# TensorE in source order: projections taken in set numbers between the steps of linear attention and attention

## The chip, the cores and the metric

The kernel runs on one core of one Trainium2 chip. TensorE (PE) multiplies, VectorE (DVE), ScalarE (ACT) and GpSimd (POOL) work element by element, SyncE (SP) and the other queues start DMAs. Each engine takes its instructions in the order in which they stand in its own queue and waits on semaphores for the others. The metric is the time of one execution on the device in microseconds; a kernel's time is the median of its runs. Beside it stands one profiled execution, from which all rows below come.

## The reference

A two-layer encoder for one sequence of 512 tokens with 16 learned meta tokens ahead of them (528 in all, width 1024). Each layer is a feed-forward half step, a mixer and another half step; the mixer runs gated linear attention and softmax attention side by side and merges them by gates.

```python
for l in range(DEPTH):                     # DEPTH = 2
    h = h + 0.5 * swiglu(rmsnorm(h, g[l, 0]), gate[l, 0], up[l, 0], down[l, 0])
    h = h + mixer(rmsnorm(h, g[l, 1]), w_in[l], ...)
    h = h + 0.5 * swiglu(rmsnorm(h, g[l, 2]), gate[l, 1], up[l, 1], down[l, 1])
return rmsnorm(h, final_norm)[:, N_META:]

def mixer(z, ...):
    q_a, k_a, v_a, r_a, lr_f, lr_b, q_b, k_b, v_b, g_a, g_b = split(z @ w_in)
    a = gla_branch(...)        # 4 heads (keys 64, values 128), forwards and backwards, chunked, decay per channel:
                               # o_t = q_t . S_t,  S_t = diag(alpha_t) S_{t-1} + k_t^T v_t; RMS norm per head; * silu(r_a)
    b = attention_branch(...)  # 8 query heads, 2 key heads of 64; RMS norm of q and k, rotary positions, softmax
    y = sigmoid(g_a + b0) * (a @ w_pa) + sigmoid(g_b + b1) * (b @ w_pb)
    return y @ w_out
```

In the last layer only the 512 tokens are needed behind the mixer's keys and values.

## The kernel before

Everything is held as channels by tokens: the 1024 channels are 8 chunks of 128 partitions, the 528 tokens lie along the free dimension, and a matmul takes a 128x128 weight tile and 264 tokens (512 where only the tokens count). Each float32 product is three matmuls on split operands: `whi` (ScalarE's cast, L222) and `wlo` (the remainder, L223 on VectorE) of the weights with the same two of the activations. `Weights` keeps a plan of all tiles in order of use, fetches them in slabs of 512 KB by DMA on SyncE's queue and makes `whi` and `wlo` four slabs ahead.

Feed-forward blocks take the gate and up products in pairs of blocks by seven products in place of eight (`product_of_pair`, matmuls at L498), then the down product (`product`, L378). `Norm` prepares the next block as chunks of the residual `h` are finished: `pair` splits the operands (`xc`, L429 and L430), `square` adds up the squares (L412, L416), and `rs` takes the mean over channels on TensorE (`means`, L384) and the inverse root.

The mixer projects four `r`, the low-rank decays `lr`, and then, pair of heads by pair of heads, `q`, `k` and two `v` (`project`, matmuls at L378, evacuated by L465). `gla_pair` works on one pair: the decays for both directions (L608 to L642: a product with `w2`, exponentials and logarithm on ScalarE, cumulative sums L618 on VectorE), products of keys and queries with the decays (L644, L647, L664), transposes (L596, L651), the chunk states (L687 to L702), scores inside a chunk with their mask (L714 to L718), outputs (L723, L724, copied by L726), and the norm per head (square L731, mean L384, logarithm L390, exponential L361, then L734 and L735). `attention` projects keys, values and queries, normalises and rotates them (`rope`, L743 to L746), and its `prologue(g)` prepares one group of four query heads: means of the query squares (L796, L798), their inverse roots `rq` (L803 to L808), and the queries split into a high and a low half (L818, L819). `group` walks through 8 units a group: four score matmuls for each of two heads (L832, L833), maximum (L835), exponential (L361), scaling, transposes (L857, L867), copies (L860, L861), and products with the values (L874, L875). 16 projections for the gates end in `g` (copied by L578, scaled by L951).

The source says what is computed; the order on every engine is set by the tile framework's scheduler, which by its own costs draws matmuls of any step forward as soon as their operands and buffers allow. So projections stand between the transposes and scores where it put them. The late 12 gates of a layer take their `wlo` from POOL (`W.lo = G`) instead of VectorE, and so does the product `kp` (L645) in `gla_pair`.

Of the kernel before, what the change touches and what calls it, by code (L numbers as in the profile page):

```python
# [29 lines left out]
EARLY = 4  # L30
KINDS = ("ss", "mm", "ss", "sm")
AHEAD = 1
SLAB = 1024
# [14 lines left out]
def ffn_steps():  # L48
# [3 lines left out]
    for g, n in enumerate(GROUPS):  # L52
        steps += [("P", pair, c) for c in "1265"]
# [14 lines left out]
def weight_plan():  # L68
# [8 lines left out]
    def ffn(l, f):  # L77
        for step in ffn_steps():
            if step[0] == "P":
                plan.append(("op", (l, f)) + step[1:])  # L80
            else:
                _, g, m, first, last = step
                mat("ffn_w_down", (l, f), m * P, 2 * sum(GROUPS[:g]) + first, last - first)

    gate_cols = [c + m * P for m in range(KC) for c in (O_GA, O_GB)]
    for l in range(DEPTH):
# [8 lines left out]
        for c in gate_cols[:EARLY] + [O_KB, O_VB] + [O_QB + i * P for i in range(4)] + gate_cols[EARLY:]:  # L95
            mat("w_in", (l,), c, 0, KC)
# [153 lines left out]
def build(tc, ctx, xt, wts, win, par, w2, const, umask, out):  # L250
# [129 lines left out]

    def means(weights, x):
# [16 lines left out]
    class Norm:  # L398


        def __init__(self, gc):
            self.gc, self.x, self.acc = gc, [], None
# [14 lines left out]

        def pair(self, j):

            raw = [slot("t"), slot("t")]  # L420
            for i, t in enumerate(raw):
                S.activation(t, h(2 * j + i), AF.Identity, scale=col(self.gc + 2 * j + i))
# [26 lines left out]
        def chunk_of_pair(self, c):  # L449
            self.square(c)  # L450
            if c % 2:
                self.pair(c // 2)

# [24 lines left out]
    def ffn(l, f, norm, done, following):  # L478
# [6 lines left out]
        def product_of_pair(p, product):  # L485
# [4 lines left out]
            if begin:  # L490
                st[where] = pair(kind == "s2")
            acc = st[where][:, :, :w]
            hi, lo = W.op((l, f), p, product)
            at = PLACE[product]
            for k, (xh, xl) in enumerate(x):
                for j in range(2):
                    for i, (a, b) in enumerate(((hi, xh), (hi, xl), (lo, xh))):
                        TE.matmul(acc[:, j], a[:, j, k], b[:, at], start=bool(begin and k == 0 and i == 0),  # L498
                                  stop=k == len(x) - 1 and i == 2, skip_group_check=not begin)
# [58 lines left out]
        for i, step in enumerate(steps):  # L558
            if step[0] == "P":
                product_of_pair(*step[1:])  # L560
                if step[1:] == (0, "5"):
                    rs = norm.rs()
# [9 lines left out]
    def project(x, rs, tag, f=1.0, n=T):  # L572
        t = slot(tag, n=n)
        acc = product("w_in", Acc("mm", n), x, KC, by_half=True)
        with tc.high_priority():
            if rs is None:
                for pv, cut in acc.parts:
                    S.copy(cut(t), pv)  # L578
            else:
                scaled(t, acc, rs, f)  # L580
        return t
# [4 lines left out]
    def gla_pair(l, p, lr, w2t, sr, qa, ka, va, n_out):  # L586

        prods = []
        qin = None
        dec = small.tile([P, 2, NB], F32, tag="dec", name=nm("dec"))  # L590
        kt, vk = [slot("q"), slot("q")], [slot("q"), slot("q")]
        ktm = slot("k")
        for hh in range(2):
            tp = pair()
            for b, bs, _ in blocks:
                TE.transpose(tp[:, 0, bs], va[hh][:, bs], ident)  # L596
            TE.transpose(tp[:META, 1, :P], va[hh][:, MB], ident)
            S.copy(vk[hh][:, :SEQ], tp[:, 0])
            S.copy(ktm[:META, 256 + hh * P : 256 + (hh + 1) * P], tp[:META, 1, :P])

        def blk(ap):
            return ap[:, :SEQ].rearrange("p (b t) -> p b t", b=NB)

        for d in range(2):
# [4 lines left out]
            a, g, c, ct_ = slot("t"), slot("t"), slot("t"), slot("t")  # L609
# [11 lines left out]
            mm_, mt_ = c[:, T - 1 : T].broadcast_to([P, META]), None  # L621
# [9 lines left out]
            qp, kp = slot("p"), slot("p")  # L631
            if d == 0:
                S.activation(g, a, AF.Exp, scale=-r16)
                S.activation(a, a, AF.Exp, scale=r16)
                S.activation(c, c, AF.Exp, scale=r16)
                S.activation(ct_, ct_, AF.Exp, scale=-r16)
                ein, eq, ek, eend = c, a, g, ct_
            else:
                S.activation(c, a, AF.Exp, scale=-r16)
                S.activation(a, a, AF.Exp, scale=r16)  # L640
                S.activation(ct_, ct_, AF.Exp, scale=-r16)
                S.activation(g, g, AF.Exp, scale=r16)  # L642
                ein, eq, ek, eend = ct_, c, a, g
            V.tensor_tensor(qp[:, :n_out], qa, eq[:, :n_out], ALU.mult)  # L644
            G.tensor_tensor(kp, ka, ek, ALU.mult)  # L645
            ke = slot("p")
            V.tensor_tensor(ke, ka, eend, ALU.mult)  # L647

            tp = pair()
# [8 lines left out]
            if qin is None:  # L658
                qin = [slot("p"), slot("p")]
            e0 = 127 if d == 0 else 0  # L660
            for hh in range(2):
                rows = slice(hh * HD, (hh + 1) * HD)
                to = slice(d * HD, (d + 1) * HD)
                V.tensor_tensor(qin[hh][to, :n_out], qa[rows], ein[rows, :n_out], ALU.mult)  # L664
                V.tensor_copy(dec[to, hh, :], blk(ein)[rows, :, e0])
            prods.append((qp, kp))
# [9 lines left out]

# [7 lines left out]
        for b in [NB, 0, 1, 2, 3]:  # L684
# [5 lines left out]
            if b == NB:  # L690
                S.copy(state(0)[0:HD], pv[0:HD])
            elif b < NB - 1:
                for hh in range(2):
                    V.scalar_tensor_tensor(state(nxt)[0:HD, hh], state(b)[0:HD, hh], dec[0:HD, hh, b : b + 1],
                                           pv[0:HD, hh], ALU.mult, ALU.add)
            if b != NB:
# [393 lines left out]
```

## Time and profile before

| | before |
|---|---|
| median of 3 runs (lowest to highest) | 2320.05 us (2318.82 to 2320.76) |
| profiled execution, its span | 2324.93 us, 2323.2 us |
| TensorE busy, mean granted clock | 2244.2 us (97%), 0.983 |
| VectorE, ScalarE, POOL busy | 1525.0 us, 1192.3 us, 231.8 us |
| HBM read | 264.38 MB |

The span runs from the first to the last instruction of the profile; the profiled execution's own time is 1.7 us longer and 4.9 us above the median. Layer 0's first feed-forward block lies at 34 to 390 us, its mixer to 830, the second block to 1182, layer 1's first block to 1556, its mixer to 1968, the last block to the end. Rows of instructions read: line, engine, operation, output<-inputs, shapes, count, then busy time, mean duration in ns, and the idle time before with what ended it. A duration runs from an instruction's start to its end; the next one on the same engine can start before that.

### The profile page before, as it was taken

Reading aid. Unit: us, or ns where it says so; the run is one execution under the profiler, and the core shown is the slowest. Engines: PE = TensorE matmul, PEld = TensorE weight load, DVE = VectorE, ACT = ScalarE, POOL = GpSimd, SP = SyncE. Lnnn points to the kernel's source line nnn. Section 1 sums busy time; section 2 is a strip of 40 time slices with the busy share of each in tenths; the row PEclk is TensorE's granted clock in tenths of the full one; section 3 lists DMA queues with packets and bytes.
Section 4 is the critical chain, followed back from the end, with each engine's and each line's share of the span. In section 5 each row is a group of like instructions: output and inputs, shape, how many; then the busy total and the mean of one; then the engine's idle time right before and its main releaser. Section 6 shows DMA issues by size and latency. Waiting matters only on the chain.

```text
span 2323.2 us, 39861 instructions
## 1 busy us (share of the span) xinstructions
PE 2244.2 (97%) x16548; PEld 2122.3 (91%) x16548; DVE 1525.0 (66%) x2355; ACT 1192.3 (51%) x1761; POOL 231.8 (10%) x218
## 2 busy tenths in 40 slices
PE   6999999999899999999989999999998999999997
PEld 5999999989899999999989999998787878989896
DVE  6657567566875676565676565674768767656666
ACT  7536354344784464453565353553446846636353
POOL 1111000000112010101011110100001110101010
PEclk9999999999998999999989999999999999999999
DMA  8868563111103386776658585632121135958671
GB/s 230 233 160 219 140 158 106 64 48 64 37 28 100 102 204 167 186 186 173 170 139 209 147 219 144 172 101 73 46 64 45 32 124 140 229 150 215 160 178 64
DMA packets 88412, 315.19 MB, mean 136 GB/s; under 512 B 9830, under 2 KB 12262, under 8 KB 88232
## 3 DMA queue, kind: packets, MB, share of 16 engines
q1 hardware_dynamic: 61136, 218.26, 28.4%
q0 software_dynamic: 25344, 92.29, 22.4%
q8 instruction: 130, 2.13, 0.4%
q10 hardware_dynamic: 1752, 2.11, 0.3%
q14 instruction: 50, 0.41, 0.1%
HBM read 264.38 MB, written 2.10 MB: 115 GB/s over the span
## 4 chain that ended last, share of the span: by engine, by line
PE 89%; DVE 6%; ACT 2%; issue 1%; DMA 1%; SPq 0%; DVEq 0%; POOL 0%; ACTq 0%
PE ss L498 38%; PE ss L378 27%; PE mm L378 12%; PE sm L378 3%; PE sm L857 1%; PE sm L874 1%; PE ss L714 1%; PE sm L875 1%; DVE wlo L223 1%; PE ss L832 1%; PE ss L384 1%; PE sm L687 1%; PE ss L833 1%; ACT whi L222 1%; PE sm L723 1%
## 5 line engine op out<-in xcount | busy, mean ns | idle before, releaser
L498 PE MATMUL ss<-xc,whi 128*128 128x264 f32 (+1 forms) x4928 | 902.3, 285 | 25.5 <-ACT whi L222 9.2
L498 PEld LDWEIGHTS ss<-xc,whi 128*128 128x128 f32 x4928 | 766.8, 189 | 28.1 <-ACT whi L222 9.9
L498 PE MATMUL ss<-xc,wlo 128*128 128x264 f32 (+1 forms) x2464 | 702.0, 285 | 3.5 <-DVE wlo L223 3.5
L378 PE MATMUL ss<-g,whi 128*128 128x264 f32 (+2 forms) x2668 | 494.2, 301 | 0.0
L498 PEld LDWEIGHTS ss<-xc,wlo 128*128 128x128 f32 x2464 | 466.0, 189 | 4.6 <-DVE wlo L223 4.4
L378 PEld LDWEIGHTS ss<-g,whi 128*128 128x128 f32 x2668 | 388.6, 188 | 17.4
L378 PE MATMUL mm<-x,whi 128*128 128x264 f32 (+1 forms) x1712 | 387.0, 318 | 0.1
L222 ACT CAST whi<-w 128x1024 fp32r<-128x1024 f32 (+1 forms) x221 | 230.8, 1047 | 257.9 <-PE ss L378 116.0
L222 ACT CAST whi<-raw 128x1024 fp32r<-128x1024 f32 x190 | 199.2, 1048 | 303.0 <-PE mm L378 108.0
L223 DVE TENSOR_TENSOR wlo<-w,whi 128x1024 fp32r<-128x1024 f32 (+1 forms) x221 | 267.9, 1218 | 108.5 <-ACT whi L222 106.3
L378 PE MATMUL ss<-g,wlo 128*128 128x264 f32 (+2 forms) x1334 | 310.0, 301 | 0.0
L378 PEld LDWEIGHTS mm<-x,whi 128*128 128x128 f32 x1712 | 283.3, 192 | 19.8 <-issue 2.5
L378 PE MATMUL mm<-x,wlo 128*128 128x264 f32 (+1 forms) x856 | 269.9, 320 | 0.0
L223 DVE TENSOR_TENSOR wlo<-raw,whi 128x1024 fp32r<-128x1024 f32 x166 | 203.1, 1224 | 98.6 <-ACT whi L222 97.5
L378 PEld LDWEIGHTS ss<-g,wlo 128*128 128x128 f32 x1334 | 213.4, 188 | 8.7
L223 DVE TENSOR_TENSOR wlo<-s,whi 128x1024 fp32r<-128x1024 f32 x88 | 107.6, 1223 | 101.7 <-ACT whi L222 101.7
L378 PEld LDWEIGHTS mm<-x,wlo 128*128 128x128 f32 x856 | 162.8, 192 | 11.0 <-issue 2.2
L222 ACT CAST whi<-s 128x1024 fp32r<-128x1024 f32 x88 | 92.4, 1050 | 154.1 <-PE ss L498 134.4
L465 DVE SCALAR_TENSOR_TENSOR t<-ss,rs 128x528 f32<-128x528 f32 (+1 forms) x95 | 66.0, 700 | 126.9 <-PE ss L378 126.8
L173 ACT ACTIVATE s<-w 128x1024 f32<-128x1024 f32 x88 | 93.3, 1060 | 84.6 <-DMA w<-win 47.9
L223 POOL TENSOR_TENSOR wlo<-raw,whi 128x1024 fp32r<-128x1024 f32 x24 | 57.7, 2403 | 363.0 <-ACT whi L222 279.7
L178 POOL DMA_DIRECT2D s<-win x44 | 41.1, 934 | 508.7 <-ACT s L173 508.4
(234 smaller groups left out, 2747.9 us busy)
## 6 DMA issues: line engine op xcount, KB each, us to landing
w<-win SPq DMA_DIRECT2D x219, 512.0 KB, 4.6
raw<-wts SPq DMA_DIRECT2D x190, 512.0 KB, 3.4
s<-win POOLq DMA_DIRECT2D x44, 512.0 KB, 6.8
w<-s POOLq DMA_DIRECT2D x44, 512.0 KB, 5.7
w<-win POOLq DMA_DIRECT2D x44, 512.0 KB, 6.9
s<-w POOLq DMA_DIRECT2D x44, 512.0 KB, 7.1
h<-xt SPq DMA_DIRECT2D x3, 528.0 KB, 6.6
out<-h SPq DMA_DIRECT2D x4, 256.0 KB, 2.3
```

Of the source, the lines that this page charges most:

```text
L173: self.nc.scalar.activation(t, w, AF.Copy, scale=-1.0)
L178: self.nc.gpsimd.dma_start(t, src, accum_op=ALU.add)
L222: nc.scalar.copy(hi[:, cs], w[:, cs])
L223: self.lo.tensor_tensor(lo[:, cs], w[:, cs], hi[:, cs].bitcast(F32), ALU.subtract)
L378: TE.matmul(acc.half[i][:width], lhs, rhs[:, acc.spans[i]], start=first, stop=last)
L384: TE.matmul(a, weights, x[:, hs], start=True, stop=True)
L465: V.scalar_tensor_tensor(cut(dst[rows]), pv[rows], -0.5 * f, cut(rs[rows]), ALU.mult, ALU.mult)
L498: TE.matmul(acc[:, j], a[:, j, k], b[:, at], start=bool(begin and k == 0 and i == 0), stop=k == len(x) - 1 and i == 2, skip_group_check=no ...
L687: TE.matmul(ps[:, hh * P : (hh + 1) * P], ktok(b, hh), vtok(b, hh), start=True, stop=True)
L714: TE.matmul(ats[:n, hh, d * n : (d + 1) * n], prods[d][1][rows, bs], prods[d][0][rows, bs], start=True, stop=True)
L723: TE.matmul(os_, vtok(b, hh), t3[:, hh], start=True, stop=False)
L832: TE.matmul(s[:n, i, :HF], lhs, kh[:, hs], start=True, stop=False)
```

## The change

TensorE alone is put under `manual_schedule`: its instructions now issue in the order of the source; the other engines are still ordered by the scheduler. In the source, `project` becomes `projection`, a generator that yields after each matmul, and `Stream` runs 30 of them a layer (24 matmuls of 264 or 512 tokens in each half). `pump(n)` issues the next n matmuls (a 512-wide one counts two), and `get` runs the stream until a projection is done. `gla_pair`, `keys_values` (the keys' and values' part of `attention`) and `attention` call `pump` with set numbers; in the attention units `share()` spreads what is left over 96 across the units. The decays are a function of their own (`gla_decays`): those of pair 1 are computed in the middle of pair 0, ahead of its norm. Keys and values come before pair 1; all 16 gates come last. The splits of both branches' outputs move into the units of the second group (`between`). The `wlo` of the late gates and `kp` come back from POOL to VectorE, each half of a projection is evacuated by itself, the first two products behind a norm (`products_late`, and the first pair of a feed-forward block) take the last operand's matmuls last, and `chunk_of_pair` squares a chunk after its operands are split.

```diff
-    def project(x, rs, tag, f=1.0, n=T):
-        t = slot(tag, n=n)
-        acc = product("w_in", Acc("mm", n), x, KC, by_half=True)
...
+    def projection(key, x, rs, f=1.0, n=T):
+        cost = 2 if n == SEQ else 1
+        def run():
...
+                        TE.matmul(a, lhs, rhs[:, hs], start=k == 0 and i == 0, stop=k == KC - 1 and i == 2)
+                        if (k, i) != (KC - 1, 2):
+                            yield cost
+                with tc.high_priority():
+                    if rs is None:
+                        S.copy(t[:, hs], a)
+                    else:
+                        V.scalar_tensor_tensor(t[:, hs], a, -0.5 * f, rs[:, hs], ALU.mult, ALU.mult)
+                yield cost
+            return t
+        return key, run, cost * 3 * KC * (1 if n == SEQ else 2)
...
+    class Stream:
+        def pump(self, n):
+            while n > 0 and (self.current or self.jobs):
+                if self.current is None:
+                    key, run, _ = self.jobs.pop(0)
+                    self.current = key, run()
+                try:
+                    done = next(self.current[1])
+                    n -= done
+                    self.left -= done
+                except StopIteration as end:
+                    self.out[self.current[0]] = end.value
+                    self.current = None
...
+    def gla_decays(p, lr, w2t, pump):
...
+            pump(8)
+        return out
...
-            G.tensor_tensor(kp, ka, ek, ALU.mult)
+            V.tensor_tensor(ek, ka, ek, ALU.mult)
...
+        last()
+        sqs = []
         for hh in range(2):
-            hd = 2 * p + hh
             sq = slot("t", n=n_out)
             S.activation(sq, o[hh], AF.Square)
+            sqs.append(sq)
+        for hh, sq in enumerate(sqs):
+            hd = 2 * p + hh
+            pump(12)
             y = slot("t", n=n_out)
             rsqrt_of(means(o128, sq), y, False)
...
         def prologue(g):
...
+            pump(16)
+            with tc.high_priority():
+                ms = pair()
+                for c, sq in enumerate(sqs):
...
+        def share():
+            n = max(0, stream.left - KEPT) // (2 * turns[0])
+            turns[0] = max(1, turns[0] - 1)
+            return n
...
+                turn = share()
+                pump(turn)
                 for c2 in range(2):
                     tp = sm()
...
+        pump(16)
+        decays = [gla_decays(0, lr, w2t, pump)]
+        pump(12)
+        qa, ka, va, vb = stream.get("q0", "k0", "v0", "w0")
+        pump(12)
+        gla_pair(0, decays[0], sr, qa, ka, (va, vb), n_out, pump, lambda: decays.append(gla_decays(1, lr, w2t, pump)))
+        qa, ka, va, vb = stream.get("q1", "k1", "v1", "w1")
+        kt, vt = stream.get("kb", "vb")
+        pump(12)
+        vs = keys_values(l, kt, vt, pump)
+        stream.get("qb0")
+        gla_pair(1, decays[1], sr, qa, ka, (va, vb), n_out, pump, lambda: None)
+        qt = stream.get(*[f"qb{i}" for i in range(4)])
...
-        W.lo = G
-        gates += [project(x, None, "g", n=n_out) for _ in range(2 * KC - EARLY)]
-        W.lo = V
...
         def chunk_of_pair(self, c):
-            self.square(c)
+            self.gained(c)
             if c % 2:
                 self.pair(c // 2)
+            self.square(c)
...
-        build(tc, ctx, out=out, **aps)
+        with tc.manual_schedule(engines={mybir.EngineType.PE}):
+            build(tc, ctx, out=out, **aps)
```

Three places show what this does to the order. The first is TensorE at the start of attention in layer 0. Before, from the last means of the query squares (L796, L798; `t` is a square) to the first scores (L832; `k` the keys, `p` the split query); 85 rows of L378, projections into `mm`, stand between them, of which the first and last two are shown:

```order
L796 MATMUL ss_6209<-const,t_6217 128x2 x4
L798 MATMUL ss_6209<-t_6217,const 128x16
L378 MATMUL mm_6085<-x_4066,wlo_5816 128x264
L378 MATMUL mm_6085<-x_4119,whi_5815 128x264
...
L378 MATMUL mm_6145<-x_4273,whi_5969 128x264
L378 MATMUL mm_6145<-x_4272,wlo_5970 128x264
L832 MATMUL ss_6268<-k_6202,p_6245 128x264
```

The same place now, where L907 and L909 are the means, L943 and L944 the scores, and L640 is a projection:

```order
L640 MATMUL mm_6006<-x_4003,whi_5591 128x264
L907 MATMUL ss_6058<-const,t_6037 128x2 x4
L909 MATMUL ss_6058<-t_6037,const 128x16
L907 MATMUL ss_6058<-const,t_6039 128x2 x4
L909 MATMUL ss_6058<-t_6039,const 128x16
L943 MATMUL ss_6113<-k_6030,p_6090 128x264
L944 MATMUL ss_6113<-k_6031,p_6090 128x264
```

No projection stands between the means and the scores any more; the next one comes behind the first 16 score matmuls.

The second is ScalarE at the norm of pair 0 in layer 0. Before, the squares (L731), the two logarithms (L390) and exponentials (L361) of the norm stand nearly together (`k` is an output of linear attention, `ss` a mean):

```order
L731 ACTIVATE t_5077<-k_5000 128x528
L390 ACTIVATE t_5079<-ss_5080,eps 128x528
L731 ACTIVATE t_5087<-k_5001 128x528
L361 ACTIVATE t_5079<-t_5079 128x528
L222 CAST whi_5277<-raw_5163 128x1024
L390 ACTIVATE t_5089<-ss_5090,eps 128x528
```

Now, where L821 squares, L669 to L693 are decays of pair 1 (`p`), and L435 and L366 are logarithm and exponential:

```order
L821 ACTIVATE t_5379<-k_5142 128x528
L670 ACTIVATE p_5305<-p_5305 128x528
L671 ACTIVATE p_5305<-p_5305 128x528
...
L690 ACTIVATE p_5306<-p_5305 128x528
L692 ACTIVATE p_5308<-p_5308 128x528
L691 ACTIVATE p_5305<-p_5305 128x528
L693 ACTIVATE p_5307<-p_5307 128x528
L670 ACTIVATE p_5347<-p_5347 128x528
L435 ACTIVATE t_5394<-ss_5395,eps 128x528
L671 ACTIVATE p_5347<-p_5347 128x528
L366 ACTIVATE t_5394<-t_5394 128x528
L435 ACTIVATE t_5414<-ss_5415,eps 128x528
```

The first logarithm has moved behind five steps of the first direction's decays and two of the second's.

The third is TensorE where layer 1's first feed-forward block begins. Before, the mean over channels (L384) stands inside the first product of the new block (L498), behind 11 of its matmuls:

```order
L378 MATMUL ss_13311<-g_12911,wlo_13014 128x264 x2
L498 MATMUL ss_13388<-xc_13058,whi_13135 128x264
...
L498 MATMUL ss_13388<-xc_13117,whi_13135 128x264
L384 MATMUL ss_13526<-t_13034,const 128x264 x2
L498 MATMUL ss_13388<-xc_13116,wlo_13136 128x264
```

Now, the mean being L429 and the products L551:

```order
L551 MATMUL ss_13476<-xc_13341,whi_13375 128x264
L551 MATMUL ss_13476<-xc_13342,whi_13375 128x264
L551 MATMUL ss_13476<-xc_13341,wlo_13376 128x264
L429 MATMUL ss_13512<-t_13022,const 128x264 x2
L551 MATMUL ss_13522<-xc_13041,whi_13398 128x264
```

It has moved behind four whole products, 96 matmuls, of which the first 36 don't need the last two chunks of the residual (`xc_13341`, `xc_13342`).

234 lines of the change are left out of this document (148 added, 86 removed).

## The prediction

> **What bounds the kernel now.** I read the page first, then busy time by stage, then TensorE's waits, then the granted clock, and only then single instructions.
>
> ```profile
> span 2323.2 us, 39861 instructions
> PE 2244.2 (97%) x16548; PEld 2122.3 (91%) x16548; DVE 1525.0 (66%) x2355; ACT 1192.3 (51%) x1761; POOL 231.8 (10%) x218
> ```
>
> ```profile
> 34.00:390.00 356.00, 356.00 (x2918) 355.89 (x2917) 226.82 (x285) 175.12 (x214) 34.71 (x40) 1.00 0.67 176
> 436.00:550.00 114.00, 107.81 (x757) 96.39 (x756) 73.41 (x158) 47.03 (x98) 7.18 (x4) 0.93 0.15 48
> 550.00:740.00 190.00, 180.30 (x1357) 169.99 (x1356) 138.91 (x301) 126.50 (x262) 28.83 (x12) 0.96 0.16 51
> 1602.00:1715.00 113.00, 107.22 (x632) 87.86 (x631) 78.19 (x163) 50.56 (x97) 7.75 (x4) 0.95 0.16 52
> 1715.00:1860.00 145.00, 136.78 (x786) 111.62 (x785) 112.47 (x236) 101.14 (x201) 21.62 (x9) 0.99 0.15 48
> ```
>
> TensorE is busy in 97% of the span, and in the first feed-forward block (34 to 390 us) in all of it, at full clock. Those blocks keep their order inside, so they cannot gain. The last four rows are linear attention and attention of the two layers (length, busy PE, PEld, DVE, ACT, POOL, then PE clock). There TensorE stands still for 6.2 + 9.7 + 5.8 + 8.2 = 29.9 us, and by the clock column it loses about half of the time below full clock: (0.07 x 114) + (0.04 x 190) + (0.05 x 113) + (0.01 x 145) = 22.7 us. So 52.6 us is what the stages that the change reorders lose by standing and by clock. The waits say on whom:
>
> ```profile
> PE ss L651 <- DVE p L647: 11.8, 8, 2.0
> PE ss L498 <- ACT xc L429: 7.3, 1, 7.3
> PE sm L857 <- DVE q L861: 6.6, 5, 2.0
> PE ss L384 <- DVE t L416: 5.4, 3, 2.7
> PE ss L832 <- DVE uq L806: 3.4, 2, 1.9
> ```
>
> They are small and spread: the longest of the mixers (third column) is 2.0 us. L498 and L384 belong to the borders between blocks.
>
> ```profile
> 513.20:530.20 17.00, 17.00 (x67) 13.39 (x66) 6.55 (x21) 2.61 (x9) 0.00 (x0) 0.50 0.00 1
> 700.90:711.10 10.20, 10.20 (x46) 9.95 (x46) 0.94 (x6) 4.63 (x12) 0.00 (x0) 0.50 0.08 30
> ```
>
> ```profile
> 699.95 0.33 PE L857 MATMUL sm<-const,t 64*128 64x64 f32 x2 [1.23 <-DVE q L861]
> 1194.95 2.13 PE L384 MATMUL ss<-t,const 128*128 128x264 f32 x4 [2.67 <-DVE t L416]
> ```
>
> The clock halves for 10 to 17 us at a time, once after a wait of only 1.23 us in a thin stretch (699.95).
>
> **The change part by part.** The matmuls stay the same; what changes is what stands between them.
>
> *Borders between blocks.* Before, the mean (L384) stands behind 11 matmuls of the next block and waits 2.7 us for the last square. Now the squares come after the operands, and 96 matmuls stand ahead of it: at the pace of this row,
>
> ```profile
> 539.37 9.83 PE mm L378 x81
> ```
>
> 121 ns each, that is 11.6 us of cover for a chain that was 2.7 us late. I let all three waits (5.4 us) go, and 1.6 us of the half clock that follows the longest of them: -7.0. The 7.3 us ahead of L498 stay: that wait is for a bank of PSUM that VectorE frees, and nothing is taken out of VectorE's queue ahead of it. If the squares came late all the same, the price is the 7.0.
>
> *Coarser blocks.* Before, a scheduler drops single projection matmuls between transposes; now they come in eights and more. In PE's order 45 changes of matmul kind and 16 of tile go. Each costs something like the step from
>
> ```profile
> 690.55 0.29 PE L378 MATMUL mm<-x,whi 128*128 128x264 f32 x1
> 690.89 0.66 PE L857 MATMUL sm<-const,t 128*128 128x128 f32 x4
> ```
>
> 0.34 us where 0.12 is the pace: 0.2 us, so up to 12 us; some of these gaps lie under waits, and I take half, -6.0.
>
> *The old waits of the mixers.* A fixed order with projections between the steps can cover all 52.6 us; it also leaves TensorE with nothing to issue wherever the number of projections set at a step is too small. So I follow the new order and sum what VectorE and ScalarE have queued ahead of each operand. The largest place is the start of attention. Before, 85 projection matmuls (10.3 us) stand between the last mean of the queries (L798) and the first scores (L832), and the wait left is 1.9 us. Now none stands there, and 28 stand between the first mean of linear attention's output and those of the queries. VectorE's queue there, with its groups in before:
>
> ```profile
> L734 DVE SCALAR_TENSOR_TENSOR t<-k,par,t 128x528 f32<-128x528 f32 x4 | 3.1, 764 | 0.1
> L735 DVE TENSOR_TENSOR e<-e,t 128x528 f32<-128x528 f32 x4 | 2.8, 708 | 0.1
> L743 DVE STREAM_SHUFFLE t<-i 128x528 f32<-128x528 f32 x6 | 4.5, 750 | 0.0
> L744 DVE SCALAR_TENSOR_TENSOR i<-i,par,const 128x528 f32<-128x528 f32 x6 | 4.5, 755 | 0.0
> L745 DVE SCALAR_TENSOR_TENSOR t<-t,par,const 128x528 f32<-128x528 f32 x6 | 4.6, 760 | 0.0
> L746 DVE TENSOR_TENSOR i<-i,t 128x528 f32<-128x528 f32 x6 | 4.2, 698 | 0.0
> L618 DVE TENSOR_TENSOR_SCAN t<-const,t 128x128 f32<-128x128 f32 x16 | 5.6, 405 | 0.1
> ```
>
> ```profile
> L390 ACT ACTIVATE t<-ss,eps 128x528 f32<-128x528 f32 x6 | 4.2, 702 | 4.4 <-PE ss L384 4.4
> L361 ACT ACTIVATE t<-t 128x528 f32<-128x528 f32 x6 | 3.9, 652 | 0.0
> ```
>
> ```profile
> 564.76 1.05 PE L796 MATMUL ss<-const,t 128*128 128x2 f32 x8
> ```
>
> Two of each of the six wide ones, and two operations of their kind on 64 partitions (the split of the keys and of the first query), are 14 operations of about 0.73 us, 10.3 us; one cast (0.43) and 11 narrow ones (0.17 each) make 12.6 us. It starts 1.35 us (L390 + L361) after the first mean. TensorE brings against it 28 x 0.121 and the means of the queries, about 1.0: 4.4 us. So 1.35 + 12.6 - 4.4 = 9.6 us of waiting. But durations overlap on one engine:
>
> ```profile
> 575.59 0.70 DVE L746 TENSOR_TENSOR i<-i,t 128x528 f32<-128x528 f32 x1
> 576.21 0.17 DVE L821 CAST qm<-p 128x16 fp32r<-128x16 f32 x1
> 576.32 0.17 DVE L813 TENSOR_TENSOR i<-i,rq 128x16 f32<-128x16 f32 x1
> ```
>
> ```profile
> 481.05 0.63 ACT L731 ACTIVATE t<-k 128x528 f32<-128x528 f32 x1
> 481.58 0.63 ACT L361 ACTIVATE t<-t 128x528 f32<-128x528 f32 x1
> ```
>
> From start to start the wide VectorE operation takes 0.62 us where its duration is 0.70, the narrow one 0.11 where it is 0.17, and ScalarE's 0.53 where it is 0.63. By starts the queue is 14 x 0.65 + 0.35 + 11 x 0.1 = 10.5 and the wait 1.2 + 10.5 - 4.4 = 7.3 us. I take the starts; the durations are the upper end.
>
> The other places in layer 0, summed the same way (by durations; by starts):
> - Second mean of pair 0: its bank is free only after the first mean's logarithm, which stands on ScalarE behind the decays of pair 1. From the product that starts them: Square, Abs and two exponentials (2.5 us), on VectorE one wide step, four scans (1.6) and two more (3.8 in all), then six ScalarE steps (3.9): 10.2 us, against 40 matmuls of 0.121 and two products of the decays, 5.9. It waits 4.2; by starts 2.7.
> - Keys and values: the second pair of transposes waits for ScalarE copies behind the splits of the values. After the keys' norm VectorE has 4.3 us queued (three wide steps, an evacuation, a weight split of 1.22, a split), then both engines 1.5 more; TensorE brings 1.5: 4.3. The first pair waits 2.1 for that norm, a half bank 0.9: 7.3; 5.7.
> - Start of linear attention, projections waiting for VectorE to empty a half bank behind decays and weight splits, and the first state, one or two wide steps each: 3.2; 2.2.
> - Means of pair 1 and of the queries: 2.6; 1.8.
> - First softmax (reduction, exponential, scaling past 18 matmuls), and the second head group's preparation: 6.2; 4.2.
> - 16 attention units at about 0.4 us: 6; 3.5.
>
> With the start of attention (9.6; 7.3) that is 39 and 27 us. Behind a waiting matmul stand only projections of gates, and who waits for those (copies on ScalarE) has slack; the waits cost their length and no more. Layer 1 has no meta tokens in its queries and about 4 us less: 35 and 23. TensorE arrives later at each wait than its dense pace says, by the switches still left (0.2 us each); I take 4 us off. So 27 + 23 - 4 = 46 us of waits, and 8 us of half clock (waits over 3 us now come about twice a layer, each with a stretch of some 3.4 us, at half loss, and its edges): 54 against 52.6, +1.4.
>
> *Work moved off POOL.* This and the unchanged widths have rows:
>
> ```profile
> L223 POOL TENSOR_TENSOR wlo<-raw,whi 128x1024 fp32r<-128x1024 f32 x24 | 57.7, 2403 | 363.0 <-ACT whi L222 279.7
> L223 DVE TENSOR_TENSOR wlo<-raw,whi 128x1024 fp32r<-128x1024 f32 x166 | 203.1, 1224 | 98.6 <-ACT whi L222 97.5
> L951 DVE SCALAR_TENSOR_TENSOR g<-g,rs 128x528 f32<-128x528 f32 x16 | 22.1, 1387 | 11.9 <-ACT g L578 11.8
> L951 DVE SCALAR_TENSOR_TENSOR g<-g,rs 128x512 f32<-128x512 f32 x16 | 13.8, 864 | 10.3 <-ACT g L578 10.2
> ```
>
> 24 weight splits (12 a layer) come to VectorE, 12 x 1.22 = 14.7 us, and four key products at about 0.7. VectorE would be busy 139 + 17 of 190 us in layer 0, less 8 if L951 falls from 1.39 to 0.86 us with POOL's splits gone from beside it. TensorE needs more than that in the stage and covers it, so I cost the move at nothing beyond the queues summed; with the cover gone it is 17 - 8 = 9 us a layer, at best a gain of a few hidden us.
>
> The sum: 2323.2 is the span, 2324.9 the profiled execution's own time. 2324.9 - 7.0 - 6.0 + 1.4 = 2313.3. The profiled execution is 4.9 us above the median of the runs (2320.05), so on their scale I predict **2308 us**.
>
> **The rivals.**
> 1. *All is covered.* Only the start of attention and the two waits of keys and values that have no projection between them stay, 7.3 + 5.9 and 3.5 x 2, some 20 us, with 3 us of half clock: -52.6 + 23 - 13 = -42.6, **2277 us**. For it: before's 85 matmuls at the start of attention are free to cover other places now. Against it: the sums above.
> 2. *The waits replace what they were to remove, in full.* The place is VectorE's one queue ahead of the first scores, and ScalarE's ahead of the second mean. By durations, 39 + 35 = 74 less 7 for the lag gives 67 us of waits, and 14 us of half clock: 81 against 52.6, +28.4 - 13 = +15.4, **2335 us**, slower. It decides from the point where mixers lose over 52.6 + 13 + 4.6 = 70 us. For it: 1.23 us of waiting was enough for 10.2 us at half clock, so the units' small waits may set it off too (6 of the 14 us). [...]
> 3. *Even.* The gains at borders and switches are real, and mixers lose some 7 to 17 us more than before: **2320 us**.
>
> **How the numbers follow.** Forecast (2290 to 2315): 0.35. All covered (below 2290): 0.17. Even, within 0.2% or 4.6 us, which is about what a measurement of this kernel can tell from no change: 0.11. Slower (over 2325): 0.37. Faster is 0.35 + 0.17 = 0.52. Since both signs hold much of the chance: the forecast's own range is 2290 to 2315, and the whole one, with a little outside each end, is 2270 to 2340.
>
> **What would show it.** In the new profile: no wait of the mean at 829, 1195 and 1966; a wait of the first scores for VectorE of 5 to 10 us in each layer, against 1.9 before; a wait of the second mean's neighbours for ScalarE of 2 to 4 us; PE busy 2230 to 2250 us. The forecast is wrong if the clock in the four stages is at 1.00 with waits below 25 us (rival 1), or if their waits together pass 60 us (rival 2).

## The result, and the profile after

The change made the kernel slower: 2395.23 us (median of 4 runs, 2393.49 to 2398.46) against 2319.44 us of before in the same runs, a ratio of 1.0331 with a 95% interval of 1.0313 to 1.0348. The forecast was 2308 us, and the time lies outside its range of 2290 to 2315, and outside the wider one as well.

The page of the changed kernel, then the stages of the mixers by busy time, with the start of layer 0's attention (554 to 568) in a row of its own (the stretches lie elsewhere than before, since the stages are longer):

```profile
span 2396.4 us, 39841 instructions
PE 2253.4 (94%) x16548; PEld 2132.2 (89%) x16548; DVE 1520.4 (63%) x2387; ACT 1192.0 (50%) x1761; POOL 159.2 (7%) x186
```

```profile
418.00:554.00 136.00, 128.32 (x990) 119.88 (x990) 85.58 (x187) 52.62 (x103) 0.00 (x0) 0.97 0.18 56
554.00:568.00 14.00, 5.71 (x44) 5.27 (x42) 11.65 (x28) 6.65 (x15) 0.00 (x0) 0.79 0.09 32
568.00:774.00 206.00, 172.85 (x1216) 161.36 (x1217) 117.80 (x268) 114.93 (x244) 0.00 (x0) 0.90 0.11 37
1615.00:1752.00 137.00, 130.86 (x854) 111.96 (x852) 87.47 (x187) 56.29 (x105) 0.00 (x0) 0.98 0.19 61
1752.00:1950.00 198.00, 160.51 (x836) 128.31 (x836) 120.03 (x252) 111.12 (x215) 0.00 (x0) 0.91 0.12 39
```

VectorE and ScalarE do the same work; TensorE stands still more. In these rows it stands for 7.7 + 8.3 + 33.2 + 6.1 + 37.5 = 92.8 us, where it was 29.9, and the clock column gives (0.03 x 136) + (0.21 x 14) + (0.10 x 206) + (0.02 x 137) + (0.09 x 198) = 48 us, where it was 22.7. The two overlap, though: the column counts half clock also where TensorE waits in it. Of 95.6 us at half clock in these rows, 27.3 us are waiting that is already in the 92.8 (the clock's record laid over TensorE's waits; before, 0.05 of 44.4 us). So the clock itself costs about (95.6 - 27.3) / 2 = 34 us, and both together 127 for 52 before, +75 us. Nearly all of it is in the two attention stretches (568 and 1752 on). TensorE's waits over the whole span:

```profile
PE sm L981 <- DVE q L974: 34.9, 24, 3.6
PE ss L943 <- DVE p L930: 15.2, 2, 8.2
PE ss L551 <- ACT snap L559: 12.9, 4, 9.9
PE sm L989 <- DVE lr L985: 12.7, 10, 4.0
PE ss L943 <- ACT t L366: 11.4, 6, 3.0
PE ss L551 <- ACT whi L227: 9.1, 2, 7.6
PE ss L551 <- DVE t L515: 8.4, 1, 8.4
PE ss L715 <- ACT k L718: 5.6, 2, 3.3
```

The first and the fourth row belong to the units of attention: the meta tokens' transposes (L981) wait for the first copy of the main transposes, and the products with the values (L989) for the copy of the meta tokens. They are 47.6 us in all. Before, the products (L874) waited nowhere, and of the transposes the main ones waited 6.6 us (L857), the meta tokens' 2.1:

```profile
PE sm L867 <- DVE e L881: 1.2, 2, 1.0
PE sm L867 <- DVE sc L842: 0.9, 1, 0.9
```

One unit on TensorE and VectorE, at 653 us (the timeline, projections L640 left out; the first row is the end of the eight main transposes, L970):

```profile
651.79 0.38 PE L970 MATMUL sm<-const,t 128*128 128x128 f32 x2
653.81 0.39 PE L981 MATMUL sm<-const,t 128*16 128x128 f32 x2 [0.55 <-DVE q L974]
656.22 0.39 PE L989 MATMUL sm<-q,k 128*128 128x256 f32 x1 [0.92 <-DVE lr L985]
```

```profile
653.07 0.69 DVE L974 TENSOR_TENSOR q<-sm,q 128x512 fp32r<-128x512 f32 x1 [0.41 <-ACT q L973]
654.01 1.23 DVE L228 TENSOR_TENSOR wlo<-raw,whi 128x1024 fp32r<-128x1024 f32 x1 [0.26 <-ACT whi L227]
655.16 0.68 DVE L974 TENSOR_TENSOR q<-sm,q 128x512 fp32r<-128x512 f32 x1
655.76 0.40 DVE L985 TENSOR_TENSOR lr<-sm,lr 16x256 fp32r<-16x256 f32 x1
```

A unit hands its transposes to ScalarE and VectorE twice, one after the other, and nine projections (1.1 us) stand behind each. The first hand-over passes no data to what waits: L981 reads the softmax. It waits for a buffer. A unit writes three tiles `sm` (two of main transposes, one of meta tokens and products) in turn into two buffers, so the third needs the first one copied: L981 starts at 653.81, when the first L974 ends (653.07 + 0.69) and the second has not begun. No run had a third buffer. The weight split L228 stands between the copies, so it was the first suspect.

The stages, cut at the starts of the last and the first gate and up matmul (L551, L498 before) on each side of a mixer, moved so: the first block's gate and up products end at 356.3 for 352.7 us (+3.6), from there through its down product and layer 0's mixer to the next block's first product it takes 509.4 for 473.2 us (+36.2), the two blocks in the middle to their last gate and up product 695.6 for 695.0 us, and layer 1's mixer, in the same way, 475.1 for 442.4 us (+32.7).

### The profile page after: what moved, and what is told of

Same layout as the page of the kernel before. It is cut to its first block, busy times and chain, and to the rows that moved or that the text cites. A ratio compares the mean times of both kernels' runs of the same rounds, so it can differ in the third digit from the quotient of the medians.

```text
span 2396.4 us, 39841 instructions
## 1 busy us (share of the span) xinstructions
PE 2253.4 (94%) x16548; PEld 2132.2 (89%) x16548; DVE 1520.4 (63%) x2387; ACT 1192.0 (50%) x1761; POOL 159.2 (7%) x186
## 3 DMA queue, kind: packets, MB, share of 16 engines
q10 hardware_dynamic: 1752, 2.11, 0.3%
## 4 chain that ended last, share of the span: by engine, by line
PE 83%; DVE 8%; ACT 5%; issue 2%; DMA 2%; SPq 0%; DVEq 0%; POOL 0%; ACTq 0%
PE ss L551 37%; PE ss L383 23%; PE mm L640 11%; PE sm L383 2%; PE mm L383 2%; DVE wlo L228 2%; PE sm L989 1%; ACT t L366 1%; ACT whi L227 1%; DMA w<-win 1%; PE ss L395 1%; PE sm L990 1%; DVE sc L946 1%; DVE q L974 1%; PE ss L943 1%
## 5 line engine op out<-in xcount | busy, mean ns | idle before, releaser
L551 PE MATMUL ss<-xc,whi 128*128 128x264 f32 (+1 forms) x4928 | 906.7, 286 | 31.9 <-ACT snap L559 12.9
L551 PEld LDWEIGHTS ss<-xc,whi 128*128 128x128 f32 x4928 | 769.9, 190 | 35.2 <-ACT snap L559 13.8
L551 PE MATMUL ss<-xc,wlo 128*128 128x264 f32 (+1 forms) x2464 | 703.1, 285 | 3.9 <-DVE wlo L228 3.9
L383 PE MATMUL ss<-g,whi 128*128 128x264 f32 (+1 forms) x2620 | 484.0, 300 | 0.0
L551 PEld LDWEIGHTS ss<-xc,wlo 128*128 128x128 f32 x2464 | 467.8, 190 | 4.8 <-DVE wlo L228 4.8
L383 PEld LDWEIGHTS ss<-g,whi 128*128 128x128 f32 x2620 | 381.1, 188 | 16.3
L640 PE MATMUL mm<-x,whi 128*128 128x264 f32 (+1 forms) x1568 | 369.5, 324 | 0.0
L228 DVE TENSOR_TENSOR wlo<-w,whi 128x1024 fp32r<-128x1024 f32 (+1 forms) x221 | 267.8, 1218 | 108.7 <-ACT whi L227 106.6
L228 DVE TENSOR_TENSOR wlo<-raw,whi 128x1024 fp32r<-128x1024 f32 x190 | 232.1, 1223 | 136.8 <-ACT whi L227 128.9
L383 PE MATMUL ss<-g,wlo 128*128 128x264 f32 (+2 forms) x1310 | 303.8, 300 | 0.0
L640 PEld LDWEIGHTS mm<-x,whi 128*128 128x128 f32 x1568 | 266.8, 196 | 18.9 <-issue 3.2
L640 PE MATMUL mm<-x,wlo 128*128 128x264 f32 (+1 forms) x784 | 255.8, 326 | 0.0
L228 DVE TENSOR_TENSOR wlo<-s,whi 128x1024 fp32r<-128x1024 f32 x88 | 107.6, 1223 | 97.6 <-ACT whi L227 97.6
L640 PEld LDWEIGHTS mm<-x,wlo 128*128 128x128 f32 x784 | 154.0, 196 | 9.5 <-issue 1.5
L178 ACT ACTIVATE s<-w 128x1024 f32<-128x1024 f32 x88 | 93.3, 1060 | 90.1 <-DMA w<-win 47.6
L183 POOL DMA_DIRECT2D w<-win x44 | 39.2, 890 | 1167.9 <-DMA w<-win 1047.3
L559 ACT COPY snap<-ss 128x528 f32<-128x528 f32 (+1 forms) x132 | 77.0, 583 | 0.5 <-PE ss L551 0.5
```

The costliest lines, as they stand in the source:

```text
L178: self.nc.scalar.activation(t, w, AF.Copy, scale=-1.0)
L183: self.nc.gpsimd.dma_start(t, src, accum_op=ALU.add)
L228: self.lo.tensor_tensor(lo[:, cs], w[:, cs], hi[:, cs].bitcast(F32), ALU.subtract)
L383: TE.matmul(acc.half[i][:width], lhs, rhs[:, acc.spans[i]], start=first, stop=last)
L559: S.copy(st[name], acc)
L640: TE.matmul(a, lhs, rhs[:, hs], start=k == 0 and i == 0, stop=k == KC - 1 and i == 2)
```

## The experiments

Twelve kernels, each against runs of before. Theory F: the fixed order as such loses the time; S: the split on VectorE; P and N: the place, or the number, of the projections; O: units that are not laid over each other; A and B: attention, or the rest.

**One part taken back: POOL again.** Edit on the changed kernel:

```diff
+        W.lo = G
         bt = attention(l, kt, vs, qt, n_out, stream, between)
...
         gates = stream.get(*[f"g{i}" for i in range(2 * KC)])
+        W.lo = V
```

> The changed kernel with one edit taken back: the low halves of the weights made during attention come from POOL again, as before the change. The changed kernel takes 2395 us; its attention units wait 34.9 us at L981, 12.7 at L989 and 11.4 at the scores for softmax. Theory S (the 1.23 us split, now on VectorE, stands between a unit's copies and is what the units wait for): these waits fall by 25 us or more, and with the half clock behind them the time comes to about 2355 to 2365 us. Theory P (too few projections stand between a unit's transposes and the matmuls that need their copies): a split taken out of a third of the units helps little, waits stay above 50 us, 2385 to 2395 us. Theory F (any fixed order loses what the scheduler spread by single matmuls): the same as P.

Measured: 2402.73 us, 1.0382 (1.0352 to 1.0412), which is 12 us slower than the change by the ratios, where no theory expected more than 2395 us. L981 waits 42.1 us, more than the 34.9, and L989 7.9. Theory S falls. (POOL makes 29 splits here, where the kernel before gave it 24, and the product `kp` stays on VectorE.)

**The other part taken back: the scheduler's order.**

```diff
-        with tc.manual_schedule(engines={mybir.EngineType.PE}):
-            build(tc, ctx, out=out, **aps)
+        build(tc, ctx, out=out, **aps)
```

> The changed kernel without the manual schedule: the source keeps its stream, decays, splits and pools, but the framework's scheduler orders TensorE again. Theory F (the fixed order as such loses the time): attention's waits go back to some 20 us and the time to 2315 to 2335 us. Theory S (the split on VectorE): the scheduler spreads the projections better, but the copies are as late as before, 2340 to 2370 us. Theory P: as F, since the scheduler puts projections where operands are late.

Measured: 2278.59 us, 0.9845 (0.9817 to 0.9874). All the rest of the change is a gain of 36 us, and the fixed order alone costs 117 us (113 by the ratios). The same stages there, and what is left of the units' waits:

```profile
418.00:554.00 136.00, 134.97 (x1072) 127.18 (x1073) 92.67 (x204) 58.62 (x116) 0.00 (x0) 1.00 0.18 60
554.00:741.00 187.00, 185.70 (x1448) 176.63 (x1447) 138.45 (x311) 126.32 (x257) 0.00 (x0) 0.99 0.18 57
1585.00:1700.00 115.00, 113.96 (x710) 95.42 (x709) 79.97 (x172) 52.61 (x104) 0.00 (x0) 1.00 0.20 65
1700.00:1860.00 160.00, 159.77 (x876) 130.82 (x875) 119.60 (x244) 109.58 (x207) 0.00 (x0) 1.00 0.19 60
```

```profile
PE sm L981 <- DVE q L974: 0.5, 2, 0.2
PE ss L943 <- DVE p L930: 0.4, 1, 0.4
```

With the same instructions TensorE stands 3.6 us in these stretches (length less busy, summed). Nor has the scheduler more to cover with: from the first scores to the last products of attention it has 557 and 564 projections in the two layers (a 512-wide one counted as two), and the changed kernel 598 and 616. So their number, theory N, is not what the fixed order lacks. Its order in a stretch of units, run lengths in brackets, shows how: scores nearly two units ahead, and the transposes of one unit around the products of another.

```
fixed:     L943/944 (8) L640 (18) L970 (8) L640 (9) L981 (2) L640 (9) L989/990 (10) L943/944 (8) ...
scheduler: L970 (4) L640 (3) L981 (2) L640 (4) L943/944 (4) L640 (7) L970 (1) L943/944 (2) L970 (3) L989/990 (10) ...
```

**Only attention in source order.**

```diff
-            bt = attention(l, kt, vs, qt, n_out, stream, between)
+            with tc.manual_schedule(engines={mybir.EngineType.PE}):
+                bt = attention(l, kt, vs, qt, n_out, stream, between)
```

(the outer `manual_schedule` removed).

> The changed kernel with TensorE's order set by the source in attention alone; ahead of it and behind it the scheduler orders, which gave 2279 us when it ordered all. Theory A (the loss of the fixed order lies in attention: its start, 19 us, its units, 59 us, and half clock): 2360 to 2385 us, less what the scheduler can draw into it of the 96 projections left for the end. Theory B (the fixed order of linear attention and of the borders costs as much): 2320 to 2340 us.

Measured: 2376.29 us, 1.0241 (1.0151 to 1.0331): +98 us on the scheduler's 2279, of the 117 (92 of 113 by the ratios). Theory A holds. L981 waits 31.0 us and L943 for L930 15.5 us, as in the changed kernel.

**The projections of a unit in other places.** First all of those ahead of the transposes moved between them and L981:

```diff
                 turn = share()
-                pump(turn)
...
-                pump(turn // 2)
+                pump(turn + turn // 2)
                 o = sm()
```

> The changed kernel with one edit: of a unit's projections, those that stood ahead of the transposes (about half of all, where TensorE waits for nothing) stand between the transposes and the matmuls of the meta tokens, L981. Their number is the same. Theory P: the wait at L981 falls from 34.9 us to under 8, part of the half clock goes, 2350 to 2365 us. Theory S: the copies come late by the same 1.23 us splits; 18 projections more are 2.2 us of cover, so L981 falls all the same, but what was hidden at the softmax side now shows at the scores or at the transposes, 2375 to 2390 us. Theory F: 2385 to 2395 us.

Measured: 2376.46 us, 1.0268 (1.0239 to 1.0298). The wait at the meta transposes went entirely; the wait at the products grew from 12.7 to 23.5 us. Theory P's fall of the wait came, its time (2350 to 2365 us) did not:

```profile
PE sm L988 <- DVE lr L984: 23.5, 24, 2.4
```

Then 18 and 18 (`pump(turn)` at both places, none ahead):

> The changed kernel (2395 us) with the same 36 projections of an attention unit in other places: none ahead of its transposes, 18 between these and the meta tokens' transposes (L981), 18 between those and the products with the values. With 27 and 9 the time was 2376 us and the second hand-over (L988 there) waited 23.5 us. Theory O (a unit makes two hand-overs to ScalarE and VectorE one after the other, each some 2.5 to 3.5 us long, and in a fixed order only what stands between covers them): both waits together fall from 47.6 us in the changed kernel to about 10 to 15, 2345 to 2360 us. Theory N (there are not enough projections in attention at all, whatever their place): the waits only move, 2370 to 2380 us.

Measured: 2366.95 us, 1.0201 (1.0119 to 1.0282). The products still wait 19.7 us. It is the lowest of the places tried, though its interval overlaps the last one's, and the gain stays at 28 us: between the two theories.

Then the next unit's scores moved between the meta transposes and the products:

> As the run with 18 and 18, and the next unit's eight score matmuls moved from ahead of the unit to the place between its meta transposes and its products with the values, ahead of the 18 projections there. Theory O: the scores (about 1 us) cover the second hand-over too, but the next unit's softmax gets only 18 projections and the products, 3.6 us, for reductions, exponentials and scaling of about 3.5 us: the waits at L981 and L989 are near zero and new ones of 0 to 1 us a unit appear at the transposes; 2335 to 2360 us. Theory N: 2370 us or more.

Measured: 2380.43 us, 1.0259 (1.0177 to 1.034). Outside theory O's range: the hand-overs wait only 3.3 us, and the next unit's transposes wait for the softmax instead, 35.3 and 11.8 us:

```profile
PE sm L969 <- ACT t L955: 35.3, 24, 4.1
PE sm L969 <- DVE t L957: 11.8, 10, 1.4
```

In a fixed order, unit by unit, the cover of 36 projections can be put at one place or the other; there are three: the two hand-overs and the softmax.

**Units laid over each other by hand.** The products of unit i move between the two halves of the transposes of unit i+1:

```diff
+                    pump(turn // 3)
+                    if c2 == 0:
+                        finish_before()
+                        pump(turn // 3)
                 o = sm()
...
-                both_rows(j, slice(b * P, (b + 2) * P), weighted(prs, P)[:, :256])
+                fin = weighted(prs, P, pending)
+                pending = lambda j=j, b=b, fin=fin: both_rows(j, slice(b * P, (b + 2) * P), fin()[:, :256])
```

> The changed kernel (2395 us) with the units of attention laid over each other by hand: the first four transposes of a unit, a third of its projections, the products with the values of the unit before, a third, the other four transposes, a third, the meta transposes. The number of projections is the same. Theory O (a unit's two hand-overs to ScalarE and VectorE, one after the other, are what a fixed order unit by unit leaves open; the scheduler lays units over each other): the waits at L981 and L989, 47.6 us, fall below 12, and of the half clock in the units most goes: 2325 to 2345 us; the start of attention keeps its 19 us. Theory N (there are too few projections in attention, wherever they stand): the waits reappear at scores, softmax or banks, 2365 us or more.

Measured: 2352.93 us, 1.0135 (1.0066 to 1.0204), 42 us less than the change with the same matmuls. The units' waits fell to 12.8 us, nearly what theory O had (below 12), but the time lies between the ranges of both theories:

```profile
PE ss L943 <- DVE p L930: 15.3, 2, 8.2
PE sm L969 <- DVE q L973: 7.3, 5, 2.5
PE sm L993 <- DVE lr L987: 5.5, 6, 2.2
```

The time fell less than expected, and the half clock did not go: its stretches sum to 131.1 us over the whole execution here, 133.3 in the changed kernel, 34.7 in the scheduler's order and 81.4 in the kernel before.

Then the start of attention as well, `pump(64)` ahead of the first scores:

> The same with 64 projections taken from the units and set between the means of the queries and the first scores, where the wait for VectorE is 15.3 us in both layers and half clock follows. The wait there falls by 64 x 0.121 = 7.7 us a layer, to about 0. If the units have cover to spare once they overlap, the time falls by 15 us and 5 to 10 of half clock: 20 to 25 below the run without. If cover is a fixed sum, the units wait for what was taken from them, and the difference is 0 to 8 us.

Measured: 2337.62 us, 1.0071 (1.0041 to 1.0101), 15 us less again, between the two cases. The wait for L930 fell from 15.3 to 2.5 us, and the half clock to 97.0 us. By hand 58 of the 117 us came back in two steps; what the rest needs is open.

**The bare price of a fixed order.** The kernel before under `manual_schedule`, its source unchanged:

> The kernel before (2319 us), TensorE in the order of its unchanged source: there projections stand in blocks ahead of each step, and nothing stands between the steps. If the fixed order's price is what is left uncovered, this is the bare price: an attention unit needs about 10 us from softmax through two hand-overs to the products, of which TensorE works 3.5, so 34 units wait some 6 us each, 200 us; linear attention's four pairs some 30 to 40 us each, 140 us; with half clock 2650 to 2800 us. The stream of the change then recovers most of it. If TensorE's own chains are short and the loss in the changed kernel comes from the stream (switches, half banks, its evacuations), this is below 2450 us.

Measured: 2700.48 us, 1.1632 (1.1547 to 1.1717). So the change's edits to the source, the stream among them, are worth some 300 us under a fixed order; they replace most of what the scheduler did, not all.

**POOL in the scheduler's order.** Before with `W.lo = G` removed, all else as it was:

> The kernel before with one part of the change alone: the low halves of the late gates' weights come from VectorE instead of POOL, all else as before, 2319 us. Theory S: VectorE's queue is late in the scheduler's order too, attention's waits grow from 18 us by 15 or more, 2335 to 2350 us. Theories P and F: VectorE has 139 us of work in 190 us of the stage and takes 15 more, and POOL no longer slows its gates' scaling (L951, 1.39 us); 2312 to 2324 us.

Measured: 2293.33 us, 0.9909 (0.988 to 0.9938): neither 15 us slower nor the same, but 21 us faster. This one edit out of the change is a gain. VectorE's rows at 550 to 740 us, first of this run, then of before:

```profile
L950 DVE SCALAR_TENSOR_TENSOR g<-g,rs 128x528 f32<-128x528 f32 x12 | 8.3, 694 | 0.0
L846 DVE TENSOR_SCALAR t<-t,sc 128x528 f32<-128x528 f32 x16 | 7.8, 489 | 0.3
L840 DVE TENSOR_TENSOR sc<-sc,rq 128x1 f32<-128x1 f32 x32 | 4.5, 145 | 0.1
```

```profile
L951 DVE SCALAR_TENSOR_TENSOR g<-g,rs 128x528 f32<-128x528 f32 x12 | 18.2, 1520 | 11.8 <-ACT g L578 11.8
L846 DVE TENSOR_SCALAR t<-t,sc 128x528 f32<-128x528 f32 x16 | 9.1, 570 | 0.3
L840 DVE TENSOR_TENSOR sc<-sc,rq 128x1 f32<-128x1 f32 x32 | 7.6, 238 | 0.1
```

With POOL's splits beside it, these three of VectorE's own instructions took longer: the gates' scaling 1520 for 694 ns, the softmax's scaling (L846) 570 for 489, even a product of one element in each partition 238 for 145 ns. All of TensorE's waits in attention (L857, L832, L378 <- x, L867; 17.6 us before) are gone but for 0.3 us. POOL's split itself is also longer than VectorE's (2403 for 1224 ns), and no run parts this from the slowing.

The same edit put back in the changed kernel's scheduled form:

> The changed kernel in the scheduler's order (2279 us) with the late gates' low halves made by POOL again. In the kernel before, taking them from POOL to VectorE gave -21 us. If the gain is that POOL's 2.4 us splits slow VectorE's instructions beside them (the gates' scaling 1.39 us against 0.69) and the parts add up, putting them back costs about +21 us: 2295 to 2305 us. If the new order of steps hides VectorE's delay, it costs 0 to 8 us: 2278 to 2287 us.

Measured: 2307.53 us, 0.9949 (0.9933 to 0.9966), 24 us slower by the ratios (0.9949 - 0.9845). The parts add up: of the 36 us that the rest of the change gains, 21 to 24 are POOL's (here with 29 splits for the 24 of before) and 12 to 15 the stream's order of steps, the evacuation by halves and the borders, which were not parted further.

**The fastest.** The scheduled form with the first norm's squares at once:

```diff
-    first.late = lambda: [first.square(c) for c in range(KC)]
+    for c in range(KC):
+        first.square(c)
```

> The changed kernel in the scheduler's order (2279 us, 0.9845 of before), with one edit taken back: the squares of the very first norm are issued at once, as before, and not behind the third product. The first feed-forward block ended 3.6 us later in the changed kernel (356.3 for 352.7 us) and also in the scheduler's order (356.0). If the late squares cost that, the block ends at about 352.7 us and the time is 2275 us, 0.983 of before; if it is the order of the first two products, nothing changes. Either way it is the candidate for a version faster than both kernels: 0.980 to 0.987 of before.

Measured: 2279.43 us, 0.9828 (0.9806 to 0.985). The first block's gate and up products end at 354.8 us for 356.0, a third of the way back to 352.7; the wait of 9.8 us for a snapshot became one of 9.0 us for the mean (L429). The time is that of the form with late squares. Both beat the kernel before by 1.5 to 1.7%, and the change by 5%.

## Why the prediction was wrong, step by step

**The bound** was read rightly: some 52 us lost by standing and clock in the mixers were there to be won, and the scheduled form has 3.6 us of standing and 3.4 us at half clock in the corresponding stretches. The fixed order made the 52 into 127.

**The step that failed** is the term "16 attention units at about 0.4 us: 6; 3.5". It measured 18.1 + 6.0 us in layer 0 and 16.8 + 6.6 in layer 1, 47.5 us for a forecast of 7 (by starts, both layers):

```profile
PE sm L981 <- DVE q L974: 18.1, 13, 3.6
PE sm L989 <- DVE lr L985: 6.0, 6, 1.4
PE sm L981 <- DVE q L974: 16.8, 11, 2.6
PE sm L989 <- DVE lr L985: 6.6, 4, 4.0
```

The prediction gives the 0.4 us no working; unlike the start of attention, the unit was not followed, and of the stage as a whole it says only that TensorE has more work than VectorE and covers it. But a unit is a chain, and what counts at each of its hand-overs is the time from the transpose to the copy's end, through two queues that also carry the next softmax and weight slabs, against the nine projections there. The moves of the projections showed that the hand-overs and the softmax compete for the cover, and the overlap by hand that the waits of the hand-overs fall to 12.8 us with the same projections.

**Half clock** was 8 us in the sum and is about 34 us (48 by the clock column that the sum went by). The sum let it come with waits over 3 us, a limit that no run shows, about twice a layer; it came 13 times in the mixers, mostly after windows with 1.5 to 2.4 us of waiting (last section). Together with the units that is some 67 of the 73 us by which the mixers lose more than the 54 of the forecast.

**POOL's work at nothing** was the second wrong step, with the other sign: -12 us in the fixed order that the prediction was about (the first run), -21 to -24 in the scheduler's. The prediction had L951's 1387 and 864 ns, and valued them by VectorE's busy time, which TensorE covers. But steps of the softmax got shorter as well (L846, L840), and 17.3 us of TensorE's waits in attention went with it; that these went through the shorter steps is likely, not shown apart.

**Right** were the places followed by hand. The first scores wait 8.2 and 7.0 us for VectorE (forecast 7.3 and 5.9 by starts, 9.6 by durations), the second mean's logarithm 2.2 (2.7), and the keys' and values' transposes 8.9 in both layers together (some 10). First softmax and the second group's preparation were undersized: 8.2 us in layer 0 for 4.2 by starts and 6.2 by durations.

**Borders** (-7.0): no mean waits any more, but what follows does: 8.4 + 0.8 us at the second border where it was 7.3 + 2.7, 1.4 + 1.3 for 1.4 and 0.9 for 1.3 at the others. That is 12.8 for 12.7, nothing gained, and the start is 3.6 us later. **Coarser blocks** (-6.0): no run isolates them. Summing over both traces by how much each step from one matmul to the next, at full clock and without a wait, exceeds the median step of its shape gives some 65 us before and 59 after, which fits the forecast. With +75 in the mixers, -6 and the start's +3.6, the 73 us of the spans are accounted for within 1.

**Rival 2** named the mechanism (the waits replace what they were to remove) and put it at the wrong place: ahead of the first scores and the second mean it was as large as summed; its price of 15 us had the units at 12 us in both layers, and they took 47.5. What a fixed order would lose was a question for the chain of one steady unit, followed as the start of attention was.

## What to carry to other kernels

In an order written by hand, follow one steady turn of the loop as a chain, each hand-over against what stands behind it in the queue; busy times per engine don't show it, and the turn counts as often as it runs. Ask of each wait whether it is for data or for a buffer. Lay turns over each other before spreading filler. An engine that isn't on the path can come with longer instructions on the others, as POOL did here (VectorE's gates' scaling took 1520 ns with its splits, 694 without): value work moved off it by the durations beside it, not by its own busy time.

## What the runs showed of the hardware

The half clock came on a grid of 3.41 us. In the changed kernel the stretches but the last, at the program's end, measure 3.41, 6.83, 10.24, 13.65 and 17.07 us, and all begin at multiples of 3.41 us from each other. Laying TensorE's waits over this grid, 12 of the 16 windows ahead of a fall had between 1.5 and 2.4 us of waiting in them, two had all, and of the windows that stayed at full clock all but four (1.6 to 1.9 us) had under 1.5. The least of the 12 is 1.51 us, under half a window. Back to full clock came only after a window with at most 0.34 us of waiting, while windows with 0.9 us and more of it stayed at half, and so did three without any.

Waiting isn't the whole of it. The other two falls came after windows with 0.8 us of waiting (from 596.3 and 1750.0 us), and these hold the means of the query squares, 13 and 16 of the L907 with two columns each. In the scheduler's order, where TensorE stands 1.3 us in all of 554 to 741 us and the clock is 0.99 there, it fell at 579 us after a window without a wait, which holds 16 of them. So TensorE was busy by the profile there and lost its clock; what such narrow matmuls count for was not measured apart.

The second is VectorE beside POOL: three kinds of VectorE instructions ran 1.2 to 2.2 times as long where POOL split weights (570 for 489 ns, 238 for 145, 1520 for 694; the kernel before against the run without those splits, 550 to 740 us), and not when those splits were gone. One by one in the kernel before: of the 12 of L951 six overlap a split of POOL in time and took 2346 ns in the mean, the other six 694; of L846 one took 1741 ns for 492 of the rest, of L840 two 1629 for 145. The reductions L835 took 705 ns (four) for 698.
